# A transformer block pair in split float32: all weight subtractions moved to VectorE

## The chip, the cores and the metric

The kernel runs on one core of a Trainium2 chip. The metric is the device time in microseconds (us), the median of several runs. A profile is one further execution, taken by the hardware profiler; its length is called the span. The engines are named PE (TensorE), DVE (VectorE), ACT (ScalarE), POOL (GpSimd) and SP (SyncE), whose queue issues the weight loads. They run on their own and meet only at semaphores.

## The reference, cut to what matters

Two layers of a first block and then one layer of a second, on 256 tokens of width 1024, in float32:

```
for l in range(2):
    x = x + 0.5 * swiglu(rms_norm(x, ffn1_norm[l]), ffn1 gate, up, down)     # 1024 -> 2816 -> 1024
    h = rms_norm(x, mix_norm[l]) @ w_in[l]                                   # 1024 -> 2464
    ya, yb, yc, yd = neighbourhood(..), latent(..), differential(..), grouped(..)
    x = x + concatenate([ya, yb, yc, yd]) @ w_out[l]
    x = x + 0.5 * swiglu(rms_norm(x, ffn2_norm[l]), ffn2 gate, up, down)
    x = rms_norm(x, final_norm[l])
# second block
u = rms_norm(x) @ w_in_2                                                     # 1024 -> 7424
merged = ga * (pooled @ w_proj_a) + gb * (swa @ w_proj_b) + gc * (moba @ w_proj_c)
out = rms_norm(x + merged @ w_out_2)
```

`rms_norm` needs a power of -1/2 of a sum of squares for each token; the attention heads need one for each head.

## The kernel before

**The split.** A float32 product is made of three fast products. Each operand is a pair (hi, lo): hi is the value rounded to float32r, lo is the rest. x w is xh wh + xh wl + xl wh, added up in PSUM by `acc` (L342).

**The weights.** They are read once, in 403 units of up to [128, 1024] (512 KB), in the order of their use, by the class `Weights`. `load` (L185) issues the DMA of a unit from SP into one of three buffers (`st`). `cut` (L196) makes the pair: ScalarE copies `st` to `hi`, then `lo = st - hi` is done by VectorE or by GpSimd (L208, L209): GpSimd takes every third unit behind unit 20, 127 in all. There are six buffers of `hi` and six of `lo`. A new load into a buffer of `st` waits for the subtraction of the unit three before it; the copy to `hi` waits until the matmuls have read the unit six before.

**The stages.** A feed-forward part (`ffn`, L540) runs 12 projections (`proj`, L499) of 8 row tiles and a wide product (`wide`, L521) of 22 units. Between the two of a layer lies `mixers` (L713): five projections and four attention heads' groups, whose steps (scores, softmax, transposes, values, norms) are Python generators run from `tick` (L446) between matmuls: a step starts when the estimated time of TensorE has passed the time at which its inputs are thought to be ready. Those times come from the class `Clock` (L62), which adds up an assumed cost of each instruction on each engine. The waits on the chip come from the data alone. `tick` also calls `cut` when a place is free, so subtractions stand in VectorE's queue among the steps of attention. The second block is one long projection with two attention groups, then gates, then the last products.

**The powers.** `rpow` (L351): up to three columns go to GpSimd as `pow` (`r<-ms,mhalf`, 40 in all); several columns, as the head norms have, are done on VectorE by a start value and three Newton steps, each of three small instructions (`q<-ms,r`, `q<-q,r`, `r<-q,r`).

**The lines.** All calls on ScalarE, VectorE and GpSimd go through `Engine.call`, so in the profile they have the line L155, or L154 where a PSUM operand takes part (these are moved ahead in the queue by 14 places). They are told apart by their tiles: `lo<-st,hi` is the subtraction, `hi<-st` the copy.

Of the kernel before, what the change touches and what calls it, by code (L numbers as in the profile page):

```python
# [13 lines left out]
ALU = mybir.AluOpType  # L14
# [27 lines left out]
AHEAD = 14  # L42
SOLO = 20
OUT_ORDER = (4, 5, 2, 3, 0, 1, 6, 7)
# [17 lines left out]
class Clock:  # L62
    """Estimated times of the engines while the program is laid down. Only the order of issue
    rests on them; the waits themselves come from the data."""

# [34 lines left out]
    def ring(self, tag, bufs, ap):  # L100
        """A new tile of a ring takes the place of the one `bufs` before it."""
        r = self.rings.setdefault(tag, [])
        r.append(ap.tensor.name)
        if len(r) > bufs:
            old = r[-1 - bufs]
            t = max((e[2] for b in (self.writes, self.reads) for e in b.pop(old, ())),
                    default=0.0)
            self._note(self.reads, ap, t, "dma")
# [17 lines left out]
class Engine:  # L126
    """Passes calls on and keeps the engine's estimated time; what frees PSUM goes first."""

# [30 lines left out]
class Weights:  # L159
    """Weights in the order of their use: DRAM -> fp32 stage -> exact (hi, lo) float32r pair.  # L160
    Past the first units, which are waited for, GpSimd does every third subtraction."""

    UNIT = 1024

    def __init__(self, nc, act, dve, gps, clock, stage, whi, wlo):
        self.nc, self.act, self.dve, self.gps, self.clock = nc, act, dve, gps, clock
        self.stage, self.whi, self.wlo = stage, whi, wlo
        self.units, self.staged, self.ready = [], [], []
        self.here, self.cut_at = [], []
        self.got, self.ended = 0, set()  # L170

    def add(self, ap, k, n, per, cols=None):
        """ap [k*128, n] in DRAM, cut into units of `per` row tiles."""
        v = ap.rearrange("(k p) n -> p k n", p=128)
        if cols is not None:
            v = v[:, :, cols[0]:cols[1]]
            n = cols[1] - cols[0]
        k0 = 0
        for m in per if isinstance(per, list) else [per] * (k // per):
            assert m * n <= self.UNIT  # L180
            self.units.append((v[:, k0:k0 + m, :], m, n))
            k0 += m
        assert k0 == k
# [12 lines left out]
    def cut(self):  # L196
        if not self.staged:
            self.load()
        if self.staged:
            w, cols = self.staged.pop(0)  # L200
            m = w.shape[1]
            hi = self.whi.tile([128, self.UNIT], R, tag="hi", name="hi")[:, :m]
            lo = self.wlo.tile([128, self.UNIT], R, tag="lo", name="lo")[:, :m]
            self.clock.ring("hi", N_SPLIT, hi)
            self.clock.ring("lo", N_SPLIT, lo)
            self.act.activation(out=hi, in_=w, func=ACTF.Copy)
            n = len(self.cut_at)
            eng = self.gps if n > SOLO and n % 3 == 1 else self.dve  # L208
            eng.tensor_tensor(out=lo, in0=w, in1=hi, op=ALU.subtract)  # L209
            self.cut_at.append(self.clock.t[eng.name])  # L210
            self.ready.append(tuple(z.rearrange("p (k n) -> p k n", n=cols)
                                    for z in (hi, lo)))
            self.load()

    def can_cut(self):
        """Whether the next unit's place is free of reads yet to be laid down."""
        n = len(self.cut_at)
        return bool(self.units or self.staged) and all(
            i in self.ended for i in range(max(0, n - N_SPLIT), n - N_SPLIT + 1))

    def get(self):
        """(index, hi, lo) of the next unit."""
        while not self.ready:
            self.cut()
        self.got += 1
        return (self.got - 1,) + self.ready.pop(0)
# [6 lines left out]
def decoder(ctx, tc, a, out):  # L233
    nc = tc.nc
# [5 lines left out]
    def pool(name, bufs, stack=ctx, **kw):  # L240
# [5 lines left out]
    const = pool("const", 1)  # L246
    ws = Weights(nc, act, dve, gps, clock, pool("stage", N_STAGE), pool("whi", N_SPLIT),
                 pool("wlo", N_SPLIT))
# [16 lines left out]

# [1 line left out]
    for l in range(L):  # L267
# [32 lines left out]

# [1 line left out]
    def v3(ap, n):  # L302
# [39 lines left out]
    def acc(pss, xh, xl, w, j, first, last):  # L342
        """pss += x^T w with x = xh + xl, w = wh + wl; xl wl lies under float32's last bit."""
        _, wh, wl = w
        for ps, c0, n in pss:
            mm(ps, xh, wh[:, j, c0:c0 + n], first, False)
            mm(ps, xh, wl[:, j, c0:c0 + n], False, False)
        for ps, c0, n in pss:
            mm(ps, xl, wh[:, j, c0:c0 + n], False, last)

    def rpow(ss, n, inv, tag):  # L351
        """(ss * inv + eps) ** -0.5; several columns by a bitwise start and Newton steps."""
        m = stat.tile([128, n], F, tag=f"m{tag}{n}", name="ms")
        dve.tensor_scalar(m, ss, inv, EPS, op0=ALU.mult, op1=ALU.add)
        r = stat.tile([128, n], F, tag=f"r{tag}{n}", name="r")
        if n < 4:
            gps.tensor_tensor(out=r, in0=m, in1=mhalf[:, :n], op=ALU.pow)
            return r
        I = mybir.dt.int32
        dve.tensor_scalar(r.bitcast(I), m.bitcast(I), -0.5, float(0x5f3759df), op0=ALU.mult,  # L360
                          op1=ALU.add)
        q = stat.tile([128, 16], F, tag="q", name="q", bufs=1)[:, :n]
        for _ in range(3):
            dve.scalar_tensor_tensor(out=q, in0=m, scalar=-0.5, in1=r, op0=ALU.mult,
                                     op1=ALU.mult)
            dve.tensor_tensor(out=q, in0=q, in1=r, op=ALU.mult)
            dve.scalar_tensor_tensor(out=r, in0=q, scalar=1.5, in1=r, op0=ALU.add, op1=ALU.mult)
        return r
# [28 lines left out]
    def trans_split(hi, lo, src, scale=None):  # L397
        """src [128, 128 m] transposed and split into hi, lo [128, m, 128]."""
        ps = psT()
# [17 lines left out]
    def timed(f, *args):  # L417
        """f's result, and the time at which the last of its ops ends."""
        before, clock.last = clock.last, 0.0
# [36 lines left out]
    def drain_until(cond):  # L456
        """Background steps alone until cond holds; a step that is not due is brought forward."""
        while not cond():
# [9 lines left out]
    class Norm:  # L468
        """Residual update of one token tile, then the next projection's operand: x^T times the
        gains, which stand by feature in `gain`; the token's factor comes with the results."""  # L470

# [27 lines left out]
    def proj(K, n, per, evac, skew=False):  # L499
        """[256, 128 K] x [.., n <= 512]; evac(t, ps) takes each token tile's result."""  # L500
        ps = [psM() for _ in range(2)]
# [22 lines left out]
    def wide(order, hi, lo, blocks, evac, before=None):  # L524
        """[256, 128 len(order)] x [.., 1024]. A block of row tiles is done for token tile 0,
        then for token tile 1."""
        nk = len(order)
# [43 lines left out]

# [1 line left out]
    att = {"busy": False, "pt": 0}  # L573

    def softmax_pv(jobs, post, scored=None, have_v=lambda: True):
        """jobs: dict(t, nk, qk=[(lhsT, rhs)] * 2, bias=[ap] * 2 or None, v=[[ap] * nk] * 2, y).
        Two score tiles per job: two heads, or with `nlam` the two maps of a differential head;
        two such jobs share one value tile. Software pipeline: scores, transposes, values, out."""
        n = len(jobs)
# [135 lines left out]
    def mixers(l, cols, rows, nlam, norm_out):  # L715
# [76 lines left out]
        def qk_transposed(u, new, colq, colk, scale, hd, free=None):  # L792
            """Head norms and transposes of q (256) and k (256), split; both gains go on q."""
            qcol = stat.tile([128, 1], F, tag="qcol", name="qcol")
# [285 lines left out]

    # ================= block 1 =================
    gains = const.tile([128, 9, 8], F, name="gains")
# [41 lines left out]

    # ================= block 2 =================
    one = pool("one", 1)
# [28 lines left out]

    # MoBA: one block of 256 keys, so the selected slots are all masked
    def ev_cq(t, ps):
# [69 lines left out]
    def pooling():  # L1227
        """Windowed means less x, as a product with a constant band over the tokens."""
        pT = [v3(gates[1][:, t, 512:1024], 128) for t in range(2)]
# [215 lines left out]
```

## Time and profile before

| | |
|---|---|
| time of three runs | 1350.02, 1353.05, 1357.20 us; median 1353.05 |
| profiled execution | span 1349.9 us, first to last instruction; no other time of it is given, the fastest run lies 0.1 us above it |
| TensorE busy | 1305.5 us, 97%, mean granted clock 0.986 |
| VectorE, ScalarE busy | 700.6 us (52%), 722.9 us (54%) |
| GpSimd busy | 330.8 us (25%), of which 304.7 us are 127 subtractions and 26.1 us are 40 powers |
| weights read | 220 MB, mean 164 GB/s |

Busy time is the time in which an engine has an instruction at work, also one that stands still inside; it says nothing yet on which engine is waited for. Rows of the profile begin with a line, an engine and an operation, then out<-in. The stages lie as follows: to 57 us the start, 57 to 194 the first feed-forward part, 194 to 343 the mixers of layer 0, 343 to 726 two feed-forward parts with the border of the layers at 533 to 568, 726 to 884 the mixers of layer 1, 884 to 1062 the last feed-forward part, 1062 to 1190 the attention of the second block, then its gates and products.

### The profile page before, as it was taken

What the parts mean: (1) busy time and instruction counts of PE and PEld (TensorE: products, weight loads), DVE (VectorE), ACT (ScalarE), POOL (GpSimd) and SP (SyncE); (2) the same over time, 40 slices, a digit from 0 to 9 for tenths busy, and PEclk for the clock granted to TensorE, in tenths of its full rate; (3) what the DMA queues carried; (4) which work ended last, traced back from release to release, by engine and by line L of the source; (5) the groups of instructions that cost most, each with busy time, mean ns of one, the idle gap of its engine ahead of it and who ended that gap; (6) DMA issues with size and microseconds to landing.
All of it is one profiled execution on the core that took longest, in us unless ns stands there. A gap on an engine that the chain in (4) does not pass through costs nothing.

```text
span 1349.9 us, 17823 instructions
## 1 busy us (share of the span) xinstructions
PE 1305.5 (97%) x6514; PEld 1055.0 (78%) x6514; DVE 700.6 (52%) x1488; ACT 722.9 (54%) x1223; POOL 330.8 (25%) x171
## 2 busy tenths in 40 slices
PE   8999999989999999999999998999999999999997
PEld 7788888766788888788888876788888776678876
DVE  5534338886543433644325798563442544544365
ACT  6544346756644443544435676665443456656543
POOL 0022223211222222322222321132222231122221
PEclk9999999989999999999999899999999999999999
DMA  8766547332466655566555633156656572345652
GB/s 273 213 187 188 176 149 235 112 102 64 134 203 177 197 174 170 179 203 189 179 186 166 202 108 97 45 184 193 185 184 187 174 225 80 103 130 168 212 160 78
DMA packets 109815, 221.80 MB, mean 164 GB/s; under 512 B 7456, under 2 KB 30368, under 8 KB 109728
## 3 DMA queue, kind: packets, MB, share of 16 engines
q1 hardware_dynamic: 109152, 220.04, 53.8%
q8 instruction: 51, 0.84, 0.3%
q10 hardware_dynamic: 576, 0.63, 0.1%
q14 instruction: 36, 0.29, 0.1%
HBM read 219.59 MB, written 1.05 MB: 163 GB/s over the span
## 4 chain that ended last, share of the span: by engine, by line
PE 79%; DVE 9%; DMA 5%; ACT 3%; issue 2%; POOL 1%; SPq 0%; POOLq 0%; ACTq 0%; DVEq 0%
PE mmps L336 67%; PE tps L340 6%; PE sps L336 3%; DVE lo L155 3%; PE tps L336 3%; DMA st<-in_w_in_dram 2%; DMA st<-in_ffn_w_gate_dram 2%; ACT hi L155 2%; DVE r L155 1%; DVE q L155 1%; DMA st<-in_ffn_w_up_dram 1%; DVE hss L155 1%; POOL lo L155 1%; DVE E L154 1%; ACT junk L155 0%
## 5 line engine op out<-in xcount | busy, mean ns | idle before, releaser
L155 ACT ACTIVATE hi<-st 128x1024 fp32r<-128x1024 f32 (+2 forms) x403 | 422.1, 1051 | 427.4 <-PE mmps L336 318.0
L155 DVE TENSOR_TENSOR lo<-st,hi 128x1024 fp32r<-128x1024 f32 (+2 forms) x276 | 350.1, 1271 | 474.8 <-ACT hi L155 474.3
L155 POOL TENSOR_TENSOR lo<-st,hi 128x1024 fp32r<-128x1024 f32 x127 | 304.7, 2399 | 813.7 <-ACT hi L155 746.6
L336 PE MATMUL mmps<-hi,xTh 128*128 128x512 f32 (+2 forms) x1200 | 458.0, 382 | 0.0
L336 PE MATMUL mmps<-hi,xTl 128*128 128x512 f32 (+2 forms) x1200 | 449.4, 375 | 0.2 <-DVE xTl L154 0.2
L336 PE MATMUL mmps<-lo,xTh 128*128 128x512 f32 (+2 forms) x1200 | 449.1, 375 | 0.0
L336 PEld LDWEIGHTS mmps<-hi,xTh 128*128 128x128 f32 x1200 | 229.0, 191 | 42.2 <-issue 4.5
L336 PEld LDWEIGHTS mmps<-hi,xTl 128*128 128x128 f32 x1200 | 228.9, 191 | 38.6 <-DVE xTl L154 0.6
L336 PEld LDWEIGHTS mmps<-lo,xTh 128*128 128x128 f32 x1200 | 229.0, 191 | 35.8 <-issue 0.5
L336 PE MATMUL mmps<-lo,hTh 128*128 128x512 f32 x352 | 139.9, 397 | 0.0
L336 PE MATMUL mmps<-hi,hTh 128*128 128x512 f32 x352 | 139.7, 397 | 0.0
L336 PE MATMUL mmps<-hi,hTl 128*128 128x512 f32 x352 | 116.0, 395 | 0.0
L336 PE MATMUL mmps<-hi,yT 128*128 128x512 f32 (+1 forms) x248 | 89.1, 416 | 0.0
L336 PEld LDWEIGHTS mmps<-hi,hTh 128*128 128x128 f32 x352 | 66.1, 188 | 15.8
L336 PEld LDWEIGHTS mmps<-hi,hTl 128*128 128x128 f32 x352 | 66.2, 188 | 15.5
L336 PEld LDWEIGHTS mmps<-lo,hTh 128*128 128x128 f32 x352 | 66.2, 188 | 15.0
L155 POOL TENSOR_TENSOR r<-ms,mhalf 128x1 f32<-128x1 f32 x40 | 26.1, 655 | 201.0 <-DVE ms L155 196.7
L336 PEld LDWEIGHTS mmps<-hi,yT 128*128 128x128 f32 x248 | 46.2, 191 | 11.2 <-issue 1.4
L336 PE MATMUL mmps<-lo,yT 128*128 128x512 f32 (+1 forms) x124 | 50.2, 405 | 0.0
L155 ACT ACTIVATE E<-E,nm 128x256 f32<-128x256 f32 (+1 forms) x80 | 38.2, 480 | 21.6 <-DVE nm L155 21.3
L154 ACT ACTIVATE xTh<-tps,gains 128x128 fp32r<-128x128 f32 x112 | 31.8, 374 | 23.8 <-PE tps L340 23.8
L154 DVE SCALAR_TENSOR_TENSOR fh<-mmps,r,fg 128x512 f32<-128x512 f32 (+1 forms) x48 | 32.6, 701 | 17.1 <-PE mmps L336 17.0
(173 smaller groups left out, 1099.5 us busy)
## 6 DMA issues: line engine op xcount, KB each, us to landing
st<-in_w_in_dram SPq DMA_DIRECT2D x90, 512.0 KB, 3.9
st<-in_ffn_w_up_dram SPq DMA_DIRECT2D x88, 512.0 KB, 4.4
st<-in_ffn_w_down_dram SPq DMA_DIRECT2D x88, 512.0 KB, 4.1
st<-in_ffn_w_gate_dram SPq DMA_DIRECT2D x87, 512.0 KB, 4.2
st<-in_w_out_dram SPq DMA_DIRECT2D x24, 512.0 KB, 3.6
st<-in_w_in_dram SPq DMA_DIRECT2D x8, 416.0 KB, 3.9
scratch<-in_t5b_dram SPq DMA_DIRECT2D x4, 512.0 KB, 5.3
scratch<-in_nab_dram SPq DMA_DIRECT2D x4, 512.0 KB, 7.3
```

Source lines behind the costliest of these rows:

```text
L154: return f(*args, **kw)
L155: return f(*args, **kw)
L336: nc.tensor.matmul(ps, lhsT=lhsT, rhs=rhs, start=start, stop=stop)
L340: nc.tensor.transpose(ps, src, ident)
```

## The change

The subtraction is issued on VectorE for every unit. GpSimd is left with the 40 powers. The class no longer gets GpSimd, and the estimate of the unit's end is taken from VectorE's clock.

```
-SOLO = 20
...
-    def __init__(self, nc, act, dve, gps, clock, stage, whi, wlo):
-        self.nc, self.act, self.dve, self.gps, self.clock = nc, act, dve, gps, clock
+    def __init__(self, nc, act, dve, clock, stage, whi, wlo):
+        self.nc, self.act, self.dve, self.clock = nc, act, dve, clock
...
             n = len(self.cut_at)
-            eng = self.gps if n > SOLO and n % 3 == 1 else self.dve
-            eng.tensor_tensor(out=lo, in0=w, in1=hi, op=ALU.subtract)
-            self.cut_at.append(self.clock.t[eng.name])
+            self.dve.tensor_tensor(out=lo, in0=w, in1=hi, op=ALU.subtract)
+            self.cut_at.append(self.clock.t["dve"])
...
-    ws = Weights(nc, act, dve, gps, clock, pool("stage", N_STAGE), pool("whi", N_SPLIT),
+    ws = Weights(nc, act, dve, clock, pool("stage", N_STAGE), pool("whi", N_SPLIT),
```

Comments that are left out shift the lines by one: L155 becomes L154, L154 becomes L153. Since `Clock` now sees other costs, the order of issue moves on every engine from the 21st unit on, most in the mixers. GpSimd's queue becomes one run of 40 powers.

VectorE, end of the second feed-forward part of layer 0, before. `x<-mmps,x` is the residual update of a half of a token tile, `xTl<-...` the low half of the next operand, `r<-r` the product of two powers that came from GpSimd:

```order
L154 SCALAR_TENSOR_TENSOR x<-mmps,x 128x512
L155 TENSOR_SCALAR ms<-ss 128x1
L155 TENSOR_TENSOR lo<-st,hi 128x1024
L155 TENSOR_TENSOR r<-r 128x1
L154 SCALAR_TENSOR_TENSOR x<-mmps,x 128x512
L155 TENSOR_TENSOR lo<-st,hi 128x1024
L154 SCALAR_TENSOR_TENSOR xTl<-tps,gains,xTh 128x128 x8
L155 TENSOR_SCALAR ms<-ss 128x1
```

The same place in the changed kernel:

```order
L153 SCALAR_TENSOR_TENSOR x<-mmps,x 128x512
L154 TENSOR_SCALAR ms<-ss 128x1
L154 TENSOR_TENSOR lo<-st,hi 128x1024
L154 TENSOR_TENSOR r<-r 128x1
L153 SCALAR_TENSOR_TENSOR x<-mmps,x 128x512
L154 TENSOR_TENSOR lo<-st,hi 128x1024
L153 SCALAR_TENSOR_TENSOR xTl<-tps,gains,xTh 128x128 x8
L154 TENSOR_TENSOR lo<-st,hi 128x1024
L154 TENSOR_SCALAR ms<-ss 128x1
```

Up to the update of the last half nothing moved; the subtraction that GpSimd had stands behind the `xTl`.

VectorE, mixers of layer 0, the head norms of the latent heads amid the softmax of the differential heads, before:

```order
L155 TENSOR_REDUCE hss<-scratch 128x4
L155 TENSOR_SCALAR nm<-mx 128x2
L155 TENSOR_TENSOR q<-q,r 128x8
L155 SCALAR_TENSOR_TENSOR r<-q,r 128x8
L155 SCALAR_TENSOR_TENSOR q<-ms,r 128x8
L155 TENSOR_TENSOR q<-q,r 128x8
L155 SCALAR_TENSOR_TENSOR r<-q,r 128x8
L155 TENSOR_TENSOR qe<-qe,r 128x384
```

The Newton steps of the same norms in the changed kernel:

```order
L154 TENSOR_TENSOR q<-q,r 128x8
L154 TENSOR_TENSOR lo<-st,hi 128x1024
L154 TENSOR_SCALAR nm<-mx 128x2
L154 SCALAR_TENSOR_TENSOR r<-q,r 128x8
L154 TENSOR_TENSOR lo<-st,hi 128x1024
L154 SCALAR_TENSOR_TENSOR q<-ms,r 128x8
L154 TENSOR_REDUCE hss<-scratch 128x4
L154 TENSOR_TENSOR q<-q,r 128x8
```

Two subtractions now stand between the steps of one Newton chain, where there was none.

## Rows read from the trace of the kernel before

**Rows 1.** The page, part 1: busy us, share, instructions of each engine.
```profile
PE 1305.5 (97%) x6514; PEld 1055.0 (78%) x6514; DVE 700.6 (52%) x1488; ACT 722.9 (54%) x1223; POOL 330.8 (25%) x171
```

**Rows 2.** Stretches: length, busy us of PE, PEld, DVE, ACT, POOL, clock, DMA.
```profile
194.00:343.00 149.00, 138.25 (x789) 107.71 (x787) 115.86 (x404) 98.41 (x246) 30.02 (x21) 0.94 0.40 119
...
726.00:884.00 158.00, 148.99 (x855) 116.67 (x855) 123.65 (x425) 107.97 (x271) 33.78 (x24) 0.97 0.39 116
884.00:1062.00 178.00, 178.00 (x847) 147.89 (x846) 71.30 (x75) 82.00 (x93) 51.89 (x22) 1.00 0.62 189
1062.00:1112.00 50.00, 46.70 (x211) 37.89 (x210) 27.43 (x44) 29.38 (x48) 15.03 (x9) 0.97 0.66 204
```

**Rows 3.** Subtractions by shape, 194 to 343 us: count | busy us, mean ns | idle before.
```profile
L155 DVE TENSOR_TENSOR lo<-st,hi 128x1024 fp32r<-128x1024 f32 x15 | 18.3, 1219 | 0.7 <-ACT hi L155 0.6
...
L155 POOL TENSOR_TENSOR lo<-st,hi 128x1024 fp32r<-128x1024 f32 x9 | 21.9, 2428 | 62.4 <-ACT hi L155 45.7 <-PE tps L340 16.7
```

**Rows 4.** Timeline, mixers of layer 0: start us, us, engine, instruction.
```profile
254.50 2.39 POOL L155 TENSOR_TENSOR lo<-st,hi 128x1024 fp32r<-128x1024 f32 x1 [13.43 <-ACT hi L155]
254.56 2.35 DVE L155 SCALAR_TENSOR_TENSOR r<-q,r 128x8 f32<-128x8 f32 x1
...
257.35 0.17 DVE L155 SCALAR_TENSOR_TENSOR r<-q,r 128x8 f32<-128x8 f32 x1
```

**Rows 5.** Timeline, border of the two blocks; in brackets the idle time before.
```profile
1069.88 1.23 DVE L155 TENSOR_TENSOR lo<-st,hi 128x1024 fp32r<-128x1024 f32 x1
...
1070.04 1.48 POOL L155 TENSOR_TENSOR r<-ms,mhalf 128x1 f32<-128x1 f32 x1 [3.31 <-DVE ms L155]
...
1071.49 2.34 POOL L155 TENSOR_TENSOR lo<-st,hi 128x1024 fp32r<-128x1024 f32 x1
1071.55 2.29 DVE L155 TENSOR_TENSOR r<-r 128x1 f32<-128x1 f32 x1 [0.44 <-POOL r L155]
...
1074.50 0.90 PE L340 MATMUL tps<-ident,x 128*128 128x128 f32 x3 [2.52 <-DVE x L154]
```

**Rows 6.** The chain that ended last, its long pieces: start us, us, what.
```profile
254.56 2.36 DVE r L155
...
265.35 2.28 DVE q L155
...
274.87 2.27 DVE ms L155
...
293.92 2.35 DVE r L155
...
808.18 3.32 DVE lo L155
...
823.77 2.34 DVE r L155
...
1082.92 2.40 POOL lo L155
...
1134.16 2.16 DVE nm L155
...
1152.51 2.23 DVE es L155
...
1303.74 2.19 DVE gate L155
...
1319.13 2.58 DVE lo L155
```

**Rows 7.** The same for instructions that touch `lo`: PE, PEld, DVE, POOL (ACT none).
```profile
194.00:343.00 149.00, 50.62 (x134) 26.58 (x134) 24.38 (x20) 23.83 (x10) 0.94 0.40 119
726.00:884.00 158.00, 56.61 (x149) 29.34 (x149) 29.02 (x22) 26.43 (x11) 0.97 0.39 116
1062.00:1190.00 128.00, 45.34 (x118) 22.71 (x118) 25.45 (x19) 21.45 (x9) 0.97 0.45 136
```

**Rows 8.** GpSimd's powers in the whole trace: min/median/max ns, first and last start.
```profile
L155 POOL TENSOR_TENSOR r<-ms,mhalf x40: 542/549/1481, 15.3 to 1345.1; 128x1 f32<-128x1 f32 x40
```

## The prediction

> **What bounds the kernel now.** I read the page's busy times first. TensorE is at work 97% of the span, VectorE 52%, GpSimd 25% [rows 1]. So only time in which TensorE stands or runs at its lower clock can be won, and the next view, the stretches, tells where that is. In the feed-forward part from 884 to 1062 us TensorE is busy 178.00 of 178.00 us at full clock, with VectorE at 71.30: nothing that VectorE gets or loses there can be seen, short of doubling it. In the mixers of layer 0 TensorE is busy 138.25 of 149 us at a mean clock of 0.94, in those of layer 1 148.99 of 158 at 0.97, and from 1062 to 1112 46.70 of 50 [rows 2]. VectorE is busy 115.86 of 149 us in the first of these, 78%. The reader is to see two kernels in one: matmul stages in which the subtractions are free, and attention stages in which VectorE decides.
>
> Next comes what a subtraction costs on either engine: 1219 ns on VectorE, 2428 ns on GpSimd [rows 3]. Then the timeline, which shows that GpSimd's subtractions are not free to VectorE. At 254.56 a Newton step on 8 columns takes 2.35 us; GpSimd had begun a subtraction of 2.39 us at 254.50. The same instruction three steps on, with GpSimd quiet, takes 0.17 us [rows 4]. The busy share of VectorE thus holds standing still. The other way about it holds too: a power that takes 549 ns in the median took 1.48 us beside a subtraction of VectorE of 1.23 us [rows 5, 8].
>
> Beside these rows, the Trainium skill, page "SBUF — State Buffer", section "SBUF: two separate sides", says that VectorE and GpSimd share one pair of ports to the memory, that it is an exclusive lock, and that a VectorE instruction with two inputs from the memory stands for the whole of a GpSimd instruction that started first. The trace agrees with it (2.35 us beside 2.39). By that rule every such stall is gone after the change, since only the short powers are left to hold the pair; by the rows alone I would say the same of the stalls on the chain, so the sum below is the same by both.
>
> The last view is the chain of waits, which says which stalls were waited for. It holds four such pieces in the mixers of layer 0 (2.36, 2.28, 2.27, 2.35 us), five in those of layer 1 (four small ones, of which the last, 2.34 us, is shown, and a subtraction of 3.32), and four in the second block: 2.16, 2.23, 2.19, 2.58 us [rows 6]. It also holds the product of powers at both borders behind a second feed-forward part (`r<-r`, 2.29 us at 1071.55, with TensorE idle 2.52 us behind it; the border at 543 us looks alike) [rows 5].
>
> **The change, part by part.** *What goes from GpSimd:* 127 subtractions. *What VectorE gets:* 127 times 1.22 us [rows 3], 155 us in all. Most lie in the matmul stages, where TensorE is at 100% and VectorE at 40% [rows 2]; one more in three units hides under the matmuls, and I cost them at nothing. If that cover were gone, each would cost 1.22 us. 10 lie in the mixers of layer 0, 11 in those of layer 1, 9 in the second block's beginning [rows 7].
>
> *Borders.* In the order of the change the row `ms, lo, r, x` is unchanged up to the update that TensorE waits for, and GpSimd's subtraction stands behind the `xTl`. So the stall goes and nothing takes its place: 2.29 less 0.17 us is 2.1 us, at two places: -4.2 us. TensorE's idle time there, 2.52 us, has room for it [rows 4, 5].
>
> *Mixers.* Stalls on the chain: in layer 0 9.26 us less 4 x 0.17, is 8.6; in layer 1 I take the four small ones at the same 8.6 and the subtraction at 3.32 - 1.22 = 2.1. Together 19.3 us. Each came with one subtraction of GpSimd, and the order shows that these now stand among the same Newton steps on VectorE: 9 x 1.22 = 11.0 us come back. Net -8.3 us [rows 3, 4, 6].
>
> *Second block.* `nm` and `es` lose 2.0 and 2.06 us, the subtraction 2.58 - 1.22 = 1.36, and the gates' sum, which has half a unit's columns and so about 0.65 us by an estimate from the 1.22, 1.5. That is 6.9 us, and four subtractions bring back 4.9: net -2.0 us [rows 3, 6].
>
> *GpSimd's subtractions that are themselves on the chain.* There are three (the one at 1082.92 is shown), each 2.40 us against 1.22. They hold back weight loads, but from 1062 to 1112 TensorE is idle only 3.3 us, of which 2.52 is the border's. So they are worth between 0 and 0.8 us; I take 0 [rows 2, 5, 6].
>
> *Powers.* 40 of them now meet 403 subtractions on VectorE and not 276. One that meets one costs 1.48 - 0.55 = 0.9 us more [rows 5, 8]. I put +1 us on the path; the bounds are 0 and 40 x 0.9 x 127/403, some 11 us if every power met one, of which few are waited for.
>
> *The order of issue.* The planner now thinks VectorE later, so attention steps move against the matmuls. No row prices that. Its bounds are the nearest rows: at best TensorE's idle time in the two mixers, 10.8 and 9.0 us, goes; at worst as much again is added [rows 2]. I take 0.
>
> All of it is -4.2 - 8.3 - 2.0 + 1 = -13.5 us. A stall that leaves a chain uncovers the next one: ScalarE has 98.41 us of work in the same 149 [rows 2], and softmax needs both in turn. The borders have proved room, the rest has not. I take the half of the mixers' and the second block's gain, -5.2. That is -4.2 - 5.2 + 1 = -8.4 us, and 1341.5 us for the span of 1349.9. The median of the three runs, 1353.05 us, lies 3.15 above this span, and I keep that distance: **1344.6 us**.
>
> **The rivals.** *Wash.* In the mixers VectorE loses 8.6 and 10.7 us of stalls on the chain and gets 10 and 11 subtractions, 12.2 and 13.4 us. If these lie on the path as often as the stalls did or a little more often, only the borders' 4.2 us are left, or less: 1349 to 1355 us. For it speaks that both are nearly equal; against it that a subtraction can stand where VectorE is not waited for, while each stall counted was.
>
> *The new kernel is slower: VectorE's queue stands behind a late copy.* GpSimd stood idle 62.4 us in front of its nine full subtractions of layer 0, VectorE only 0.7 in front of its fifteen [rows 3]. GpSimd's waiting held up nobody. A subtraction on VectorE whose `hi` is late, because its load is, holds the softmax and the Newton steps that stand behind it. If all 30 moved subtractions of the attention stages [rows 7] lie on the path without further waiting, they cost 36.6 us against 23.4 of stalls in the same stages (19.3 and `nm`, `es`): +13 us, 1366 us; it decides from 19 of the 30 on, or earlier if they wait. Against it speaks the 0.7 us: subtractions were laid down where their copy was ready.
>
> The Trainium skill, page "Perfetto Trace Analysis", section "Optimizing Scalar/DVE Operations", speaks for this rival: if VectorE is saturated, it says, giving some work to ScalarE or even GpSimd may make sense, and the change does the reverse. The trace agrees in part: 78% in the mixers is near that state, though it counts the stalls. By that rule the time would be the rival's 1366 us.
>
> *The clock comes back too.* In the mixers 6% of 149 and 3% of 158 us, 13.6 us, were lost to the lower clock [rows 2], 1.2 in place of 2.4 GHz. If the full 13.5 us are won and half of this returns with shorter idle times, the gain is 20 us: 1333 us.
>
> **How the numbers follow.** The forecast has a chance of 0.45, the clock's return 0.10, the wash 0.26, the slower case 0.19. About 0.5%, 6.8 us, is what a measurement of this kernel can tell from no change; the three runs differ by that much. Faster by over that takes most of the forecast and the clock's case: 0.50. Within it: the wash and what is left of the forecast, 0.31. Slower: 0.19. The range reaches down to the clock's case, 1333, and up into the slower case, 1360, which leaves out about 2 in 10. The forecast's own range, with none to all of the mixers' gain, is 1339 to 1350.
>
> **What would show it.** In the new trace VectorE's busy time should be near 700 + 155 less the stalls (over 23 us), some 800 us; no small instruction of VectorE should take over 2 us; GpSimd should be busy under 40 us. `r<-r` at the borders should take 0.17 us, and TensorE's idle time behind it fall from 2.52 us to under 1. The mixers' stretches should be 2 to 4 us shorter each, the feed-forward stretches the same to 1 us. The forecast is wrong if VectorE shows microseconds of waiting for `hi` in the mixers, or if TensorE's idle time there grows with the stalls gone.

## The result, and the profile after

The changed kernel takes **1329.09 us** (median of four runs, 1325.61 to 1330.07), the kernel before 1351.53 us beside it (median of four). The ratio is **0.985, interval 0.9827 to 0.9874**: faster by 1.5%, some 20 us, where 8.4 us were forecast. (The two medians alone give 0.983, inside the interval.) A second measurement further down gives 0.9825 (0.9806 to 0.9844).

The profiled execution took 1329.33 us, its span 1327.2, so the distance from span to time is 2.1 us and not 3.15. Against the span of before, 1349.9, it is 22.7 us shorter. The page, part 1, as in [rows 1]:

```profile
PE 1302.8 (98%) x6514; PEld 1049.7 (79%) x6514; DVE 792.8 (60%) x1615; ACT 722.8 (54%) x1223; POOL 27.6 (2%) x44
```

VectorE has 127 instructions more and is busy 92 us more, not 155: the stalls left its busy time. The stretches of [rows 2], between nearly the same places of the program (length, busy us of PE, PEld, DVE, ACT, POOL, clock, DMA):

```profile
194.00:334.00 140.00, 136.56 (x789) 105.86 (x787) 109.55 (x414) 97.45 (x244) 6.99 (x11) 0.96 0.41 125
718.00:873.00 155.00, 149.50 (x859) 115.51 (x858) 119.86 (x437) 107.92 (x269) 7.09 (x13) 0.98 0.40 121
873.00:1051.50 178.50, 178.37 (x845) 147.74 (x845) 93.45 (x96) 81.95 (x94) 1.46 (x1) 1.00 0.63 187
1051.50:1098.00 46.50, 45.77 (x214) 37.13 (x212) 29.85 (x49) 29.53 (x48) 3.12 (x4) 1.00 0.71 221
```

Read the third line first: the feed-forward part gave VectorE 22 us more work (93.45 against 71.30) and is as long as it was. In the first line VectorE does ten instructions more than in [rows 2] and is busy 6 us less.

Subtractions by shape in the mixers of layer 0, as in [rows 3], and GpSimd's powers, as in [rows 8]:

```profile
L154 DVE TENSOR_TENSOR lo<-st,hi 128x1024 fp32r<-128x1024 f32 x24 | 29.3, 1220 | 1.6 <-ACT hi L154 1.4
...
L154 POOL TENSOR_TENSOR r<-ms,mhalf x40: 547/548/1541, 16.0 to 1322.0; 128x1 f32<-128x1 f32 x40
```

In front of the 24 full subtractions VectorE is idle for 1.6 us in all, 1.4 of them for the copy; the 62.4 us for which GpSimd waited in [rows 3] did not come over to VectorE. Of the Newton steps of [rows 4], 60 of one kind in the whole trace (minimum, median, maximum in ns), first before, then after:

```profile
L155 DVE SCALAR_TENSOR_TENSOR r<-q,r x60: 151/164/2360, 213.1 to 834.0; 128x8 f32<-128x8 f32 x24, 128x16 f32<-128x16 f32 x12, 128x4 f32<-128x4 f32 x12, 128x6 f32<-128x6 f32 x12
```
```profile
L154 DVE SCALAR_TENSOR_TENSOR r<-q,r x60: 145/159/176, 212.9 to 820.4; 128x8 f32<-128x8 f32 x24, 128x16 f32<-128x16 f32 x12, 128x4 f32<-128x4 f32 x12, 128x6 f32<-128x6 f32 x12
```

The median is the same, the maximum fell from 2360 to 176 ns: nothing holds these steps any more. The longest of VectorE's subtractions takes 1.23 us, where the longest before took 3.40. The border of [rows 5] after the change:

```profile
1059.31 1.22 DVE L154 TENSOR_TENSOR lo<-st,hi 128x1024 fp32r<-128x1024 f32 x1
...
1059.46 1.48 POOL L154 TENSOR_TENSOR r<-ms,mhalf 128x1 f32<-128x1 f32 x1 [3.31 <-DVE ms L154]
...
1060.97 0.16 DVE L154 TENSOR_TENSOR r<-r 128x1 f32<-128x1 f32 x1 [0.44 <-POOL r L154]
...
1061.65 1.22 DVE L154 TENSOR_TENSOR lo<-st,hi 128x1024 fp32r<-128x1024 f32 x1
...
1061.79 0.66 PE L337 MATMUL tps<-ident,x 128*128 128x128 f32 x4 [0.38 <-DVE x L153]
```

The product of powers takes 0.16 us for 2.29, and TensorE idles 0.38 us behind it for 2.52. The power itself still takes 1.48: it stands beside VectorE's subtraction (the first row), as it did before.

**Where the 22.7 us are.** The stages are cut here at matmuls of the same number (a matmul into `mmps` counted from the start), so that every kernel is measured between the same amounts of weight work. This is worked out from the start times in the traces, us; "rest" is the feed-forward parts and all other pieces:

```
          start    mix0 border1    mix1 border2    att2     end    rest    span
before    226.0   131.1    61.8   178.7    19.2    80.0    44.3   608.8  1349.9
changed   225.9   123.7    60.6   175.6    15.8    73.5    42.3   609.7  1327.2
```

Mixers -10.5, borders -4.6, the second block's attention -6.5, its end -2.0, all else +0.8. The same three attention pieces as stretches, before and then after (columns as above):

```profile
226.00:357.10 131.10, 120.35 (x690) 90.37 (x689) 98.23 (x353) 89.42 (x234) 24.60 (x18) 0.93 0.35 103
738.80:917.60 178.80, 169.79 (x946) 134.04 (x945) 131.79 (x422) 116.89 (x270) 41.90 (x27) 0.97 0.43 133
1113.40:1193.40 80.00, 76.62 (x453) 53.50 (x452) 39.70 (x149) 47.54 (x130) 10.91 (x5) 0.98 0.28 85
```
```profile
225.90:349.60 123.70, 119.42 (x690) 88.55 (x689) 94.14 (x358) 87.11 (x232) 6.18 (x10) 0.96 0.35 102
731.10:906.80 175.70, 170.07 (x946) 132.33 (x945) 129.94 (x436) 116.73 (x270) 7.45 (x12) 0.98 0.45 137
1099.00:1172.50 73.50, 73.30 (x453) 51.49 (x451) 39.65 (x153) 46.81 (x130) 0.00 (x0) 1.00 0.33 94
```

Length less busy time is TensorE's idle time: 10.8, 9.0 and 3.4 us before, 4.3, 5.6 and 0.2 after. That is 13.0 of the 17.0 us won in these pieces. The other 4.0 us are busy time: the matmuls are as many, but the granted clock rose from 0.93, 0.97 and 0.98 to 0.96, 0.98 and 1.00, so less of these pieces ran at 1.2 in place of 2.4 GHz. What TensorE waited for in the first piece, the longest three waits before and after (us in total, times, longest):

```profile
PE tps L340 <- DVE q L155: 3.4, 1, 3.4
PE sps L336 <- ACT qkT L154: 2.4, 1, 2.4
PE tps L340 <- DVE qkT L154: 2.2, 1, 2.2
```
```profile
PE sps L333 <- ACT E L153: 2.3, 4, 1.1
PE tps L337 <- ACT E L153: 0.5, 1, 0.5
PE mmps L333 <- ACT xTh L153: 0.5, 1, 0.5
```

Before, single long waits, two of the three for VectorE; after, short ones, most of them for ScalarE's exponentials.

### The profile page after: what moved, and what is told of

It reads as the page before. It is cut to its first block, busy times and chain, and to the rows that moved or that the text cites. A ratio compares the mean times of both kernels' runs of the same rounds, so it can differ in the third digit from the quotient of the medians.

```text
span 1327.2 us, 17825 instructions
## 1 busy us (share of the span) xinstructions
PE 1302.8 (98%) x6514; PEld 1049.7 (79%) x6514; DVE 792.8 (60%) x1615; ACT 722.8 (54%) x1223; POOL 27.6 (2%) x44
## 4 chain that ended last, share of the span: by engine, by line
PE 82%; DVE 6%; DMA 6%; ACT 4%; issue 1%; POOL 0%; POOLq 0%; ACTq 0%; SPq 0%; DVEq 0%
PE mmps L333 71%; PE tps L337 6%; PE sps L333 3%; PE tps L333 3%; DVE lo L154 2%; DMA st<-in_ffn_w_gate_dram 2%; DMA st<-in_w_in_dram 2%; ACT hi L154 2%; DMA st<-in_ffn_w_up_dram 2%; ACT junk L154 1%; DVE xTl L153 1%; ACT xTh L153 0%; POOL r L154 0%; DVE x L153 0%; ACT E L153 0%
## 5 line engine op out<-in xcount | busy, mean ns | idle before, releaser
L154 DVE TENSOR_TENSOR lo<-st,hi 128x1024 fp32r<-128x1024 f32 (+2 forms) x403 | 488.0, 1214 | 400.5 <-ACT hi L154 399.6
L154 ACT ACTIVATE hi<-st 128x1024 fp32r<-128x1024 f32 (+2 forms) x403 | 421.7, 1050 | 433.6 <-PE mmps L333 353.8
L333 PE MATMUL mmps<-hi,xTh 128*128 128x512 f32 (+2 forms) x1200 | 452.5, 377 | 1.3 <-ACT xTh L153 1.0
L333 PEld LDWEIGHTS mmps<-hi,xTh 128*128 128x128 f32 x1200 | 226.3, 189 | 43.2 <-issue 2.6
L154 POOL TENSOR_TENSOR r<-ms,mhalf 128x1 f32<-128x1 f32 x40 | 27.4, 688 | 1294.7 <-DVE ms L154 1294.6
L154 ACT ACTIVATE E<-E,nm 128x256 f32<-128x256 f32 (+1 forms) x80 | 38.2, 480 | 14.9 <-DVE nm L154 14.7
L153 ACT ACTIVATE fg<-mmps,r 128x512 f32<-128x512 f32 (+1 forms) x48 | 31.1, 652 | 21.7 <-PE mmps L333 21.7
L153 ACT ACTIVATE xTh<-tps,gains 128x128 fp32r<-128x128 f32 x112 | 31.7, 366 | 16.8 <-PE tps L337 16.8
L153 ACT ACTIVATE PT<-tps 128x512 f32<-128x512 f32 (+1 forms) x56 | 27.9, 502 | 22.0 <-PE tps L337 21.5
```

The costliest lines, as they stand in the source:

```text
L153: return f(*args, **kw)
L154: return f(*args, **kw)
L333: nc.tensor.matmul(ps, lhsT=lhsT, rhs=rhs, start=start, stop=stop)
```

## The experiments

Two theories. *Port* (LOCK in the first expectations): GpSimd's subtractions hold VectorE; that costs where VectorE is waited for, and nothing elsewhere. *Rivals*: the gain comes from the planner's other order (PLAN), or from loads whose buffers come free earlier (SUPPLY). The change does three things at once: subtractions leave GpSimd, VectorE gets them, and the planner's order moves. Ratios are to the kernel before. The stages of all runs, as in the table above, each from one execution (e10 is the changed kernel again, e11 is e1 again; a mixer of theirs differs by up to 3.5 us from the first time, so less than that says little of a single mixer):

```
          start    mix0 border1    mix1 border2    att2     end    rest    span
e1        223.2   119.6    60.2   174.5    15.8    73.2    42.5   610.3  1319.4
e2        224.2   132.1    62.7   184.4    19.5    76.6    43.6   609.7  1352.9
e3        225.3   121.8    60.2   176.0    15.8    77.0    46.5   610.7  1333.2
e4        226.4   130.5    64.4   185.8    19.1    77.1    47.9   611.1  1362.3
e5        225.4   119.4    62.9   174.9    15.8    73.8    41.9   609.0  1323.1
e6        228.6   134.5    60.3   185.1    19.5    79.7    43.8   610.3  1361.7
e7        224.7   121.3    59.1   177.5    15.8    72.3    42.5   607.7  1320.9
e9        225.9   132.1    59.9   186.9    15.7    71.1    42.4   612.4  1346.3
e10       226.9   125.1    60.6   173.9    15.8    73.4    42.4   609.9  1327.9
e11       224.8   119.4    60.1   171.0    15.8    73.3    42.5   610.1  1317.0
e12       224.7   118.6    63.0   171.4    15.8    73.3    42.1   608.5  1317.3
e13       227.6   131.0    60.3   181.2    15.8    74.2    42.5   609.2  1341.9
```

### e1 and e2: the engine without the plan, the plan without the engine

e1 takes the kernel before and issues GpSimd's third on VectorE, while the planner is still charged for GpSimd:

```
-    ws = Weights(nc, act, dve, gps, clock, ...
+    ws = Weights(nc, act, dve, Engine(nc.vector, "pool", clock, tc), clock, ...
```

> All subtractions on VectorE, but the planner's clock charges every third unit to GpSimd as in the kernel before, so TensorE's order stays near that kernel's (309 of 6266 places differ, against 793 in the change). Theory LOCK (GpSimd's subtractions hold VectorE's instructions; TensorE's idle time and its half clock follow from that): like the change, 1326 to 1334 us. Theory PLAN (the gain beyond the borders comes from the new order of issue): 1340 to 1347 us, since only the stalls of the chain go. Theory SUPPLY (the gain comes from subtractions of 1.2 in place of 2.4 us, which free the load's buffer sooner): 1326 to 1334 us as LOCK.

Measured: 1321.06 us, ratio 0.9802 (0.9767 to 0.9837). e2 does the reverse, the third stays on GpSimd and the planner is charged for VectorE: `Engine(nc.gpsimd, "dve", clock, tc)`.

> Every third subtraction is on GpSimd as before, but the planner charges it to VectorE, so TensorE's order is near the changed kernel's (180 of 6266 places differ). LOCK: like the kernel before, 1345 to 1356 us. PLAN: 1330 to 1338 us. SUPPLY: 1345 to 1356 us.

Measured: 1362.88 us, ratio 1.0095 (1.0057 to 1.0132). Both times miss what I expected of LOCK, e1 by 5 us below and e2 by 7 above; the kernel before took 1347.69 us beside them, 4 less than beside the changed kernel. So the order is not where the gain is from: the new order with GpSimd at work is slower than the kernel before, the old plan without GpSimd is the fastest of the four. By e2 and the changed kernel (1.0095 and 0.985), the move of 127 subtractions is worth 2.45% at the new plan, some 33 us; by the kernel before and e1, 2.0% at the old one, some 27.

### e3 and e4: GpSimd's stalls put back, with nobody waiting for GpSimd

To the changed kernel, GpSimd work is added whose result nobody reads: `hi - hi` into a spare tile, at every third unit. VectorE keeps all its subtractions; the order on the other engines is the changed kernel's, row by row. e3 does it from the second block on (24 units), e4 at all 127.

```
             self.dve.tensor_tensor(out=lo, in0=w, in1=hi, op=ALU.subtract)
+            if n > 20 and n % 3 == 1:
+                self.nc.gpsimd.tensor_tensor(out=self.spare[:, :m], in0=hi.bitcast(F),
+                                             in1=hi.bitcast(F), op=ALU.subtract, saturate=False)
```

> The changed kernel, plus 24 subtractions hi - hi of GpSimd into a tile that nobody reads, at the units of the second block where GpSimd subtracted before. The order on the other engines is the changed kernel's to the last place. LOCK: most of what the second block won behind its border (9.2 us by the traces) is given back: 1335 to 1341 us. PLAN and SUPPLY: 1327 to 1331 us, as the change.

> As e3_lock_in_block2, but at all 127 units that GpSimd had; to make room, the unused results of the sums of squares and of these subtractions are stored in 8 bits. Nothing waits for the added work but GpSimd's powers behind it. LOCK: the whole gain is given back and more, since VectorE keeps all subtractions: 1346 to 1360 us. PLAN and SUPPLY: 1328 to 1335 us.

Measured: e3 1335.6 us, ratio 0.9911 (0.9878 to 0.9944); e4 1367.16 us, ratio **1.0145** (1.011 to 1.018). In e3 the second block's attention goes from 73.5 to 77.0 and its end from 42.3 to 46.5, and no stage ahead of it is longer by more than half a us. e4 costs 2.95% over the changed kernel, some 40 us, more than the whole change won and 7 us above what I expected. No load and no copy to `hi` waits for GpSimd in its trace, so it isn't buffers that GpSimd holds longer. In its trace the border of [rows 5] reads:

```profile
1082.03 1.48 POOL L154 TENSOR_TENSOR r<-ms,mhalf 128x1 f32<-128x1 f32 x1 [3.31 <-DVE ms L154]
1083.48 1.89 POOL L209 TENSOR_TENSOR spare<-hi 128x1024 fp8e4<-128x1024 f32 x1
1083.54 1.84 DVE L154 TENSOR_TENSOR r<-r 128x1 f32<-128x1 f32 x1 [0.44 <-POOL r L154]
...
1086.04 0.66 PE L342 MATMUL tps<-ident,x 128*128 128x128 f32 x4 [2.05 <-DVE x L153]
```

An instruction on one column, which takes 0.16 us alone, ends with GpSimd's (1.84 beside 1.89), and TensorE idles 2.05 us again. So the engines don't meet at semaphores alone, as the opening has it: this instruction had its inputs and stood all the same. This is the port theory shown: one can take GpSimd's result away and the price stays. The Trainium skill, page "SBUF — State Buffer", section "SBUF: two separate sides", says that the pair of ports is an exclusive lock for the whole instruction; this trace agrees with it (1.84 us beside 1.89).

### e5 and e6: in which stages

The changed kernel's plan, with GpSimd doing every third subtraction of one half of the program: in e5 the 80 units cut in the feed-forward parts, in e6 the 47 of the attention stages and of the second block.

```
+            late = 69 <= n < 101 or 231 <= n < 263 or n >= 327
-            eng = self.gps if n > SOLO and n % 3 == 1 else self.dve
+            eng = self.gps if n > SOLO and n % 3 == 1 and not late else self.dve     # e5
+            eng = self.gps if n % 3 == 1 and late else self.dve                      # e6
```

> The changed kernel's plan and order, but GpSimd again does every third subtraction of the units that are cut in the feed-forward stages (80 of the 127); the 47 of the attention stages and of the second block stay on VectorE. Port theory (GpSimd's subtractions cost because VectorE stands while they run, and that is seen only where VectorE decides): feed-forward stages the same to 1 us, the borders give back some 2 us each, the second block's beginning the same; ratio to the kernel before 0.986 to 0.991. Rival, supply (a subtraction of 2.4 us holds the load's buffer longer, wherever it is): the price goes by units, 80 of 127 of the 2.45% between this plan with and without GpSimd's subtractions, so 0.985 + 0.0155 = about 1.000.

> The other half: the changed kernel's plan, GpSimd does every third subtraction of the 47 units that are cut in the mixers and in the second block, VectorE all others. Port theory: nearly all of the 2.45% comes back, ratio to the kernel before 1.002 to 1.008. Rival, supply by units: 0.985 + 47/127 of 2.45% = about 0.994.

Measured: e5 1325.09 us, ratio **0.9818** (0.9796 to 0.9841); e6 1359.38 us, ratio **1.0078** (1.0049 to 1.0107). e6 is as expected, e5 is 0.4% faster than that. 80 of the 127 subtractions on GpSimd cost nothing (the border of the layers alone is 2.3 us longer: TensorE's wait of 2.5 us for `x` is back there), the other 47 cost all. e5 has the changed kernel's order but for 4 of TensorE's 6514 matmuls. In e6, as in e2, some 320 stand at other places, so its loss may hold some of the order's; e4, where none does, shows the loss without that doubt. Supply by units, which had asked for 1.000 and 0.994, is out. The three attention pieces of e6:

```profile
228.60:363.10 134.50, 119.86 (x691) 87.60 (x690) 98.46 (x359) 89.57 (x235) 25.24 (x20) 0.96 0.35 101
744.40:929.50 185.10, 172.34 (x946) 133.48 (x945) 133.43 (x426) 117.13 (x270) 32.18 (x23) 0.97 0.43 131
1125.80:1205.60 79.80, 76.26 (x453) 53.43 (x451) 39.66 (x148) 46.76 (x130) 11.90 (x5) 0.96 0.29 85
```

TensorE's idle time is 14.6, 12.8 and 3.5 us, 30.9 in place of the changed kernel's 10.1.

### e7 and e9: what a subtraction costs on VectorE

e7 leaves the 127 moved subtractions out (for those units the products use `hi` in place of `lo`; the planner is charged as before):

```
+            if n > 20 and n % 3 == 1:
+                self.clock.op("dve", 65 + 1.04 * m, [lo], [w, hi])
+                lo = hi
+            else:
                 self.dve.tensor_tensor(out=lo, in0=w, in1=hi, op=ALU.subtract)
```

> The changed kernel with the 127 moved subtractions left out altogether (the low part of every third unit past the 20th is replaced by its high part in the products, so the output isn't the reference's; the planner is still charged for them, and matmuls and loads are as many as before). It prices the moved subtractions. By the prediction's own terms they cost 11.0 + 4.9 us in the attention stages: 1.2% under the changed kernel, ratio to the kernel before 0.973. By the revised reading, most of them fit where VectorE isn't waited for: some 5 to 7 us, ratio about 0.980 to 0.981. If every one of the 30 in the attention stages were on the path, 36.6 us: 0.958.

e9 is e4 with `nc.vector` for `nc.gpsimd`: the same 127 spare subtractions, on VectorE.

> The changed kernel with 127 more subtractions on VectorE (hi - hi into a spare tile, at the same units at which an earlier experiment put them on GpSimd, which took 1.0145 of the time before). Port theory with cheap subtractions on VectorE: some 5 to 10 us over the changed kernel, ratio 0.989 to 0.993, so some 2% under the version with the same 127 on GpSimd, though GpSimd has nothing else to do and nobody waits for the result. If VectorE's queue is what counts (the slower rival of the prediction): 30 x 1.22 = 37 us and more over the changed kernel, 1.012, as dear as on GpSimd.

Measured: e7 1325.64 us, ratio **0.9826** (0.9799 to 0.9853), some 3 us under the changed kernel's 0.985 and equal to its second measurement, 0.9825; the intervals are 0.2% to 0.3% to either side. VectorE has 145 us less to do (648.0 us busy) and the kernel gains next to nothing. Its attention pieces:

```profile
224.70:346.00 121.30, 117.21 (x690) 86.24 (x689) 87.38 (x354) 87.42 (x234) 5.73 (x11) 0.99 0.34 105
724.90:902.50 177.60, 173.14 (x946) 134.32 (x945) 115.02 (x412) 116.80 (x270) 7.45 (x12) 0.96 0.44 136
1093.70:1166.00 72.30, 72.28 (x453) 51.55 (x451) 34.02 (x148) 47.03 (x130) 0.00 (x0) 1.00 0.35 99
```

TensorE's idle time is 4.1, 4.5 and 0.0 us, 8.6 against 10.1: with the moved subtractions it is 1.5 us more.

e9: 1348.5 us, ratio **1.0004** (0.9985 to 1.0023). I had expected 0.989 to 0.993. Beside e4 the same work on VectorE is cheaper by 1.4%, and all of that lies at the borders and in the second block (59.9, 15.7, 71.1 and 42.4 against 64.4, 19.1, 77.1 and 47.9 us). In the mixers it is as dear as on GpSimd: 132.1 and 186.9 us. About half of what these are longer than the changed kernel's is idle time of TensorE (4.7 and 4.9 us), the rest busy time at a clock of 0.95. So the first moved third is nearly free and a second is not. Whether that is VectorE's queue or the order isn't told apart here: the scheduler also lays e9's attention steps out otherwise, and e13 shows what an order can do. e7 too has another order than the changed kernel in the mixers, so its 0 to 3 us are a price to within such effects.

### e10 to e13: the plan

e10 is the changed kernel once more; e11 is e1 once more; e12 is the kernel before with only the 47 `late` units issued on VectorE, the planner charged as before; e13 issues all on VectorE and charges the planner with all of them (past the 20th) on GpSimd.

> The changed kernel once more, beside the candidates on the same chip: 0.983 to 0.987 of the kernel before. By what the experiments show so far its mixers of layer 0 fell by 7.4 us with 10.2 us at the lower clock in them; if that half-speed time is chance and not part of the program, another execution shows another amount of it and a time of that stage between 119 and 125 us.

> All subtractions on VectorE, the planner charged as before the change (every third to GpSimd). If the old plan is better by the 7 us that the first runs show: ratio 0.978 to 0.982, its interval below that of the changed kernel in the same call. Rival: the two plans are equal and the 0.5% was scatter: both 0.981 to 0.986 with intervals over each other.

> The old plan with only the 47 units of the attention stages and the second block moved to VectorE; GpSimd keeps its 80 in the feed-forward stages. Port theory: these 80 cost nothing but the borders' 2 us, so 0.979 to 0.984, the same as with all on VectorE. Rival: the second border and the start pay for them: 0.985 or more.

> All subtractions on VectorE, but past the 20th the planner is charged all of them on GpSimd, so that it thinks VectorE free and lays attention steps earlier. If a plan that thinks VectorE idler is what helped: 0.975 to 0.980. Rival, that the plan is chance: anywhere from 0.978 to 0.990.

Measured side by side: e10 1325.69 us, 0.9825 (0.9806 to 0.9844); e11 1321.09 us, 0.9805 (0.978 to 0.9829); e12 1321.66 us, **0.9796** (0.9777 to 0.9816); e13 1344.22 us, 0.9956 (0.9939 to 0.9973). e10 lies just under what I expected, and e11 fits neither of its two cases. The old plan stays ahead by 4 to 5 us, but e11's interval overlaps that of e10, so a lead of 0.2% to 0.5% is likely and not shown. e11 and e12 agree that the 80 subtractions of the feed-forward parts may be on either engine. e13 is the surprise, outside both of its cases: a planner that thinks VectorE idle gives back three quarters of the gain. The two mixers of e11, then of e13:

```profile
224.80:344.20 119.40, 114.92 (x691) 85.02 (x690) 94.78 (x356) 87.25 (x231) 7.30 (x10) 0.99 0.36 106
725.00:896.00 171.00, 165.35 (x945) 128.64 (x944) 130.39 (x436) 116.95 (x270) 9.22 (x12) 1.00 0.46 141
```
```profile
227.60:358.60 131.00, 122.74 (x684) 89.67 (x683) 94.51 (x357) 85.57 (x226) 7.02 (x11) 0.93 0.32 96
739.90:921.20 181.30, 169.33 (x946) 130.19 (x946) 132.07 (x436) 117.36 (x270) 8.67 (x12) 1.00 0.44 133
```

The same VectorE work (94.78 and 94.51 us in layer 0), no stall by GpSimd, and TensorE's idle time is 4.5 and 5.7 us in one, 8.3 and 12.0 in the other. The rest of the 11.6 and 10.3 us between them is busy time, in layer 0 at a clock of 0.93 for 0.99. e11 and the changed kernel, on the other hand, have the same idle time (10.4 and 10.1 us over three pieces) and differ in the clock, 0.99 and 1.00 in the mixers against 0.96 and 0.98.

## Why the prediction was wrong in size

The direction and the mechanism were right, the size was not: -8.4 us forecast, -22.7 in the trace. By the pages TensorE's idle time fell from 44.4 to 24.4 us and its busy time by 2.7. By the prediction's own terms:

- **Borders, -4.2.** Measured -1.2 and -3.4, together -4.6. The stall went as forecast: TensorE's wait for `x` fell from 2.5 to 0.4 us at each border. At the first a wait of 1.2 us for `fh` came up in its place; at the second the granted clock rose from 0.91 to 1.00 and busy time fell by 1.3 us. That the sum is right is in part luck.
- **"9 x 1.22 = 11.0 us come back", and "four subtractions bring back 4.9".** This is the step that failed. I set every stall against a subtraction at full price because both stood among the Newton steps, 15.9 us in all. e7 prices all 127 at some 0 to 3 us. A subtraction in VectorE's queue delays a chain only if the chain's next step is ready and TensorE has nothing else; a stall counted on the chain was, by the way it was counted, already such a case.
- **"I take the half of the mixers' and the second block's gain", -5.2.** "The borders have proved room, the rest has not" was an argument, no row, and [rows 2] showed 10.8 and 9.0 us of TensorE idle in the mixers. Taken of a net that was too small, the half made it smaller still. Of the stalls themselves it was not far off: 23.4 us of them stood on the chain in the three attention pieces (19.3 and 4.1 for `nm` and `es`), and 13.0 us of idle time went there. The uncovered chain was there too, waits for ScalarE's exponentials, with 2.8 us in the first piece. Half of all stalls behind the borders, 26.2 us, with nothing set against them, gives -4.2 - 13.1 + 1 = -16.3.
- **All stalls at full price**, 30.4 us (19.3 + 6.9 + 4.2), less 3 for the subtractions and 1 for the powers, would be -26.4, and the old plan without GpSimd, at 0.9802 and 0.9805, won some 26 us. That agreement is luck: of the 26.2 us that e11 won in the three attention pieces, 12.7 are idle time, and 13.5 are busy time at a clock of 0.99, 1.00 and 1.00.
- **Second block, -2.0 full, half of it taken.** Measured -6.5 in its attention and -2.0 at its end, of which 3.2 and 1.7 us are idle time. The stalls alone, 6.9 us, were nearer than the net.
- **Order of issue, 0, bounds +-19.8.** With GpSimd at work the new order costs 0.95% (e2). Without it the changed kernel is 3 to 7 us behind the old plan (e10 and e11; e1), but the intervals of e10 and e11 overlap, so a cost isn't shown there. The bounds were fair: e13's order costs 1.5% against e11's.
- **Powers, +1.** Their sum went from 26.1 to 27.4 us, 1.3 us in all, on the path or not.
- **Feed-forward parts, 0.** Right: +0.9 us over all of "rest", and e5 shows that there it doesn't matter which engine subtracts.
- **The clock's return**, a rival at 0.10: it did come, as 4.0 us of busy time in the attention pieces and 1.3 at the second border. It belonged into the forecast in part, and not only into a rival. That the rival's 1333 us lie near the measured 1329.09 is luck: it adds 6.8 us of clock to the full net, and the kernel won 20.0 us of idle time.

The rivals: *Wash* is out, since subtractions came back far below the price of the stalls. *Slower by a late copy* is out: 24 full subtractions in the mixers of layer 0 stood behind 1.6 us of idle time in all. Its rule, the Trainium skill, page "Perfetto Trace Analysis", section "Optimizing Scalar/DVE Operations", was half quoted: the same paragraph adds that GpSimd and VectorE share a read port, so that moving work between those two might not help. e6 agrees with that half: with GpSimd's 47 subtractions in the attention stages the kernel takes 2.3% more than the changed one, in whose first such piece VectorE is busy 76% (94.14 of 123.7 us).

Of what the prediction said would show it, VectorE's 792.8 us (some 800), GpSimd's 27.6 (under 40), no small instruction over 2 us, and TensorE's 0.38 us at the border (under 1) came out. The mixers, "2 to 4 us shorter each", came out at 7.4 and 3.1.

**What stays open.** Why e13's mixers take 10 to 12 us more than e11's, step by step; what share of a stall comes back in a single stage (in the mixers of layer 1 10.7 us were counted and 3.1 won); whether e9's loss in the mixers is VectorE's queue or its order; and what sets the clock's part, below.

## What to carry to other kernels

Where a small VectorE instruction takes as long as the GpSimd instruction that began just before it, count those stalls on the chain of waits. Here 13.0 of 23.4 us of them came back as idle time of TensorE. Work that moves to VectorE in exchange is to be priced apart, by whether VectorE is waited for at its place; leaving it out, as in e7, is a way to measure it. Split such a change by stage: here 80 of 127 subtractions were free on either engine, and 47 made the difference. An estimate that orders the program is part of the change: the same work on the same engines lay between 0.98 and 0.9956 by what the planner was told.

## What the runs showed of the hardware

The granted clock isn't fixed by the program's order. e5 has the changed kernel's order in the mixers of layer 0 on every engine (GpSimd does nothing but powers there in both); the clock of that piece was 0.96 in the changed kernel, 0.95 in its second execution, 0.97 in e3, which up to there is the same kernel, and 1.00 in e5:

```profile
225.40:344.80 119.40, 115.20 (x690) 85.26 (x689) 93.78 (x358) 86.67 (x232) 6.20 (x10) 1.00 0.36 105
```

TensorE's idle time is 4.2 us here and 4.3 in the changed kernel; the whole difference, 123.7 against 119.4 us, is busy time, 119.42 against 115.20. The place where the two part, in the same form, the changed kernel first and then e5:

```profile
280.00:286.70 6.70, 4.96 (x29) 3.51 (x27) 6.44 (x29) 4.81 (x15) 0.00 (x0) 1.00 0.32 103
286.70:290.10 3.40, 3.33 (x11) 2.85 (x12) 2.40 (x14) 1.51 (x6) 0.00 (x0) 0.50 0.00 0
```
```profile
280.00:286.70 6.70, 4.88 (x26) 3.29 (x25) 6.63 (x32) 5.28 (x16) 0.00 (x0) 1.00 0.26 83
286.70:290.10 3.40, 3.34 (x23) 2.37 (x23) 3.28 (x19) 2.57 (x9) 0.00 (x0) 1.00 0.00 0
```

TensorE had been busy 4.96 of 6.7 us in the one and 4.88 in the other; then the clock fell to half, 1.2 GHz, in the first (11 matmuls in 3.4 us) and stayed at 2.4 GHz in the second (23). So 4 us of one stage, 0.3% of the kernel, hang on something that isn't in the piece's order of instructions and that no run here isolates, and differences of that size between two kernels can't be read as theirs from one profile.
